# A diffusion step's modulation vectors: from matmuls on TensorE to products on GpSimd and row sums on ScalarE

## The chip, the core and the metric

The kernel runs on one core of a Trainium2 chip. The metric is the device time of one execution in microseconds; a kernel's time is the median of its runs. The trace of the kernel before is one profiled execution on the same kind of core.

## What is computed

One step of a two-layer network over 640 tokens (512 latent, 128 context) of width 1024, all in float32. Each layer begins with six modulation vectors of 1024 numbers, once for the latent tokens (cond = c) and once for the context tokens (cond = c_ctx):

```
m = silu(cond) @ w_ada + b_ada                    # (1024) @ (1024 x 6144)
sh1, sc1, g1, sh2, sc2, g2 = split(m, 6)
h = rms_norm(x) * (1 + sc1) + sh1
x = x + g1 * mixing(h)                            # projection, three branches, W_o
h = rms_norm(x) * (1 + sc2) + sh2
x = x + g2 * swiglu(h)
```

The mixing is one projection of h (6688 columns), gated linear attention, a short convolution, a Fourier mixing, and three gated output projections that are added. The outputs are the normed x of all tokens and the final attention states of the context.

## The kernel before, in words

Activations lie with the channels on the 128 partitions, in tiles of 128 x 640, which come from one pool of 47 "units" (`N_UNITS`). Weights come from HBM in blocks of up to 128 x 1024 into six buffers (`raw`). Float32 products are made as three passes of a rounded type: ScalarE casts a block to its high part (`whi`, line 146), VectorE subtracts for the low part (`wlo`, line 147), and TensorE runs high by high, high by low and low by high. There are three buffers each of `whi` and `wlo`, and `prefetch` prepares two blocks ahead of the one that TensorE works on.

A layer runs through these stages. In the mixing stage 24 `pair`s of projection blocks follow one another; each makes seven products of a Strassen-like scheme out of sums of the weight blocks (VectorE, lines 168 to 174) and adds the results out of PSUM (VectorE, lines 282 to 295). Between the products, generators put in the attention heads. Then come 24 products of the three branches (`gated`, tiles `wb`), the products with W_o (`wo`), and the feed-forward part (`wu`, `wup`, `wd`), ordered by `ffn_order`.

The modulation vectors are made in pieces of 512 columns by `ada`: four loads of 512 KB, each with 8 matmuls in 32-column groups in the code (64 recorded matmuls for a piece), whose stationary operand is `cond` (128 x 32, two columns of it in use). ScalarE copies the result out of PSUM (`adas`, line 368), one transpose on TensorE (line 374) turns it, and VectorE adds the bias (`mod`, line 380). Four pieces, the first two vectors of layer 0, are made in `start`. Of the other 20, each layer's mixing stage makes eight (`ada_after`, at every third pair) and the feed-forward part of layer 0 makes four for layer 1. `ada_flush`, called in `tick_bg` and before the next piece, does the transpose and the bias.

The order on each engine is set by the scheduler of the tile framework from the order of the code, with data dependences, and each engine then runs its instructions in that order: an instruction that waits holds up all that stand behind it on its engine. Loads of weights are issued on SyncE's queue in the order of `make_plan`, at most six ahead.

## Time and profile before

| | us |
|---|---|
| median of three runs | 2059.89 |
| lowest and highest | 2054.49 and 2063.86 |
| profiled execution, device time | 2057.21 |
| span of its trace | 2055.4 |
| TensorE busy in the span | 1996.5 |
| VectorE busy | 1563.0 |
| ScalarE busy | 905.3 |
| GpSimd busy | 18.2 |

[...] "Busy" is the time in which at least one instruction of the engine was on record. On TensorE a record of one matmul is longer than the distance to the next, so the distance between starts says what a matmul costs in a full stream.

### The profile page before, as it was taken

How to read it: one execution, taken by the hardware profiler on the slowest of the kernel's cores; microseconds unless marked ns; L12 is line 12 of the kernel's file. 1: busy time of each engine (PE TensorE's matmuls, PEld its weight loads, DVE VectorE, ACT ScalarE, POOL GpSimd, SP SyncE). 2: the span in 40 equal slices, each digit the busy share in tenths (PEclk: the TensorE clock that was granted, in tenths of full speed). 3: DMA queues.
4: the chain of work that ended last, by engine and by line, in shares of the span. 5: the costliest groups of instructions: out<-in, count | busy, mean ns of one | idle time of the engine just before them, and what ended most of it. 6: DMA issues, size and time to landing. Idle time of an engine off the chain costs nothing.

```text
span 2055.4 us, 36451 instructions
## 1 busy us (share of the span) xinstructions
PE 1996.5 (97%) x14796; PEld 1950.0 (95%) x14796; DVE 1563.0 (76%) x2428; ACT 905.3 (44%) x1419; POOL 18.2 (1%) x52
## 2 busy tenths in 40 slices
PE   5899999999999999999999999999999999999997
PEld 4899999999999999999979999989999999999997
DVE  4778798877667777767677878898675787877876
ACT  3554435445455333333365454444543643333333
POOL 2000000000000000000000000000000000000000
PEclk9999999999999999999999999999999999999999
DMA  8243543554612343332333444335545122222221
GB/s 311 71 167 133 183 139 106 187 186 146 203 56 77 98 126 102 98 124 86 92 122 103 157 163 136 125 125 172 202 162 167 53 69 84 74 89 79 85 71 68
DMA packets 107143, 256.80 MB, mean 125 GB/s; under 512 B 13344, under 2 KB 46304, under 8 KB 106976
## 3 DMA queue, kind: packets, MB, share of 16 engines
q1 hardware_dynamic: 102528, 250.91, 37.3%
q8 instruction: 116, 1.90, 0.4%
q10 hardware_dynamic: 3728, 2.49, 0.4%
q0 software_dynamic: 720, 1.07, 0.1%
q14 instruction: 51, 0.42, 0.1%
HBM read 227.69 MB, written 26.74 MB: 124 GB/s over the span
## 4 chain that ended last, share of the span: by engine, by line
PE 83%; DVE 9%; DMA 4%; ACT 2%; issue 2%; SPq 0%; DVEq 0%; ACTq 0%
PE wd L253 14%; PE wb L253 8%; PE wo L253 3%; DMA raw<-in_w 2%; PE wu L253 2%; DVE wlo L147 2%; PE ada L362 2%; DVE S L737 1%; PE w L253 1%; ACT whi L146 1%; PE o L760 1%; PE w L235 1%; PE w L236 1%; DVE z L295 1%; PE wu L236 1%
## 5 line engine op out<-in xcount | busy, mean ns | idle before, releaser
L146 ACT CAST whi<-raw 128x1024 fp32r<-128x1024 f32 (+2 forms) x368 | 270.0, 734 | 508.2 <-PE wo L253 37.5
L147 DVE TENSOR_TENSOR wlo<-raw,whi 128x1024 fp32r<-128x1024 f32 (+2 forms) x368 | 303.9, 827 | 118.1 <-ACT whi L146 116.5
L146 ACT CAST whi<-sb 128x1024 fp32r<-128x1024 f32 x86 | 90.4, 1051 | 175.6 <-DVE sb L169 55.3
L253 PE MATMUL wd<-ffhi,whi 128*128 128x320 f32 x656 | 149.9, 310 | 0.0
L253 PE MATMUL wd<-ffhi,wlo 128*128 128x320 f32 x656 | 149.4, 309 | 0.0
L253 PE MATMUL wd<-fflo,whi 128*128 128x320 f32 x656 | 149.4, 309 | 0.0
L146 ACT CAST whi<-sc 128x1024 fp32r<-128x1024 f32 x86 | 90.4, 1051 | 96.7 <-PE wd L253 47.7
L497 DVE SCALAR_TENSOR_TENSOR x<-wd,mod,x 128x512 f32<-128x512 f32 x212 | 106.6, 544 | 18.8 <-PE wd L253 18.8
L147 DVE TENSOR_TENSOR wlo<-sc,whi 128x1024 fp32r<-128x1024 f32 x86 | 104.8, 1219 | 18.0 <-ACT whi L146 17.4
L147 DVE TENSOR_TENSOR wlo<-sb,whi 128x1024 fp32r<-128x1024 f32 x86 | 104.8, 1218 | 9.9 <-ACT whi L146 8.3
L253 PEld LDWEIGHTS wd<-ffhi,whi 128*128 128x128 f32 x656 | 109.5, 188 | 0.8 <-ACT ff L405 0.6
L253 PEld LDWEIGHTS wd<-fflo,whi 128*128 128x128 f32 x656 | 109.7, 188 | 0.0
L253 PEld LDWEIGHTS wd<-ffhi,wlo 128*128 128x128 f32 x656 | 109.6, 188 | 0.0
L168 DVE TENSOR_TENSOR sc<-raw 128x512 f32<-128x512 f32 x86 | 59.2, 688 | 41.1 <-DMA raw<-in_w 37.0
L174 DVE TENSOR_TENSOR sc<-raw,sb 128x512 f32<-128x512 f32 x86 | 59.0, 685 | 0.6
L253 PE MATMUL wb<-bhi,whi 128*128 128x320 f32 x256 | 59.3, 312 | 0.0
L169 DVE TENSOR_TENSOR sb<-sc,raw 128x512 f32<-128x512 f32 x86 | 58.9, 684 | 0.5
L170 DVE TENSOR_TENSOR sb<-raw,raw 128x512 f32<-128x512 f32 x86 | 58.8, 684 | 0.0
L253 PE MATMUL wb<-bhi,wlo 128*128 128x320 f32 x256 | 58.6, 309 | 0.0
L253 PE MATMUL wb<-blo,whi 128*128 128x320 f32 x256 | 58.3, 309 | 0.0
L362 PE MATMUL ada<-raw,cond 128*32 128x128 f32 x1536 | 49.6, 280 | 3.6 <-DMA raw<-in_w_ada 2.8
L362 PEld LDWEIGHTS ada<-raw,cond 128*32 128x32 f32 x1536 | 42.0, 112 | 10.2 <-issue 3.6
(2254 smaller groups left out, 6371.8 us busy)
## 6 DMA issues: line engine op xcount, KB each, us to landing
raw<-in_w SPq DMA_DIRECT2D x104, 512.0 KB, 4.2
raw<-in_w_ada SPq DMA_DIRECT2D x96, 512.0 KB, 4.2
raw<-in_wu SPq DMA_DIRECT2D x88, 512.0 KB, 3.6
raw<-in_wd SPq DMA_DIRECT2D x96, 192.0 KB, 2.3
sgd<-z SPq DMA_DIRECT2D x48, 320.0 KB, 2.9
sgl<-sgd SPq DMA_DIRECT2D x48, 320.0 KB, 3.6
raw<-in_wb SPq DMA_DIRECT2D x48, 256.0 KB, 2.8
raw<-in_wo SPq DMA_DIRECT2D x16, 512.0 KB, 3.6
```

The source lines that it names most:

```text
L146: self.nc.scalar.copy(hi[:, 0:n], src)
L147: self.nc.vector.tensor_sub(lo[:, 0:n], src, hi[:, 0:n].bitcast(F32))
L168: nc.vector.tensor_add(sc[:, 0:512], a21, a22)
L169: nc.vector.tensor_sub(sb[:, 0:512], sc[:, 0:512], a11)
L170: nc.vector.tensor_sub(sb[:, 512:1024], a11, a21)
L174: nc.vector.tensor_sub(sc[:, 512:1024], a12, sb[:, 0:512])
L235: nc.tensor.matmul(o, lh, rh, start=start, stop=False)
L236: nc.tensor.matmul(o, lh, rl, start=False, stop=False)
L253: nc.tensor.matmul(o[h], w[:, sl], rhs[kb][h][part], start=(kb == 0 and first), stop=(kb == nk - 1 and last))
L295: nc.vector.tensor_add(zv[:, 3:1:-1], pv(pd), zv[:, 3:1:-1])
L362: self.nc.tensor.matmul(o[32 * j:32 * j + 32], self.cond[:, kb, :], r[:, k, j], start=(kb == 0), stop=(kb == KB - 1))
L497: self.nc.vector.scalar_tensor_tensor(seg(xv), seg(v), g[:, j, i:i + 1], seg(xv), ALU.mult, ALU.add)
```

## The change

The two vectors that `start` makes stay as they were. All others are made anew. A piece is now 128 columns (one load of 512 KB) and lies differently: the 128 partitions are four quarters of the 1024 input rows times 32 output columns, and along a partition lie four column groups of 256 input rows each. For each piece, in two halves of 512 numbers, GpSimd multiplies the weights with silu(cond), once for latent into a new unit (`adp`) and once for context in place, and ScalarE runs a copy over each 256 numbers of a row with a running sum (`accum_out`). When the eight pieces of a vector are done, four small matmuls with a 0/1 matrix (`quarters`, 128 x 32, 16 columns of data) add the four quarters, and VectorE adds the bias for all eight blocks at once. There are 24 pieces in each mixing stage, one at every pair; eight in each branch stage, one at every third product; and 16 in the feed-forward part of layer 0. A piece thus has 4 GpSimd products and 8 ScalarE sums, and 80 pieces have 320 and 640; there are 10 vectors with 4 matmuls each. The flush of a finished vector stands at the next step, no longer in `tick_bg`. The pool has 46 units, and two constants are loaded at the start (`condr`, 256 KB, on ScalarE's queue with one more Silu; `quarters`, 16 KB, on GpSimd's).

```diff
@@ -43,7 +43,7 @@
 BRANCHES = [1, 0, 2]
-N_UNITS = 47
+N_UNITS = 46
 Z_BUFS = 2
@@ -61,10 +61,10 @@
     if phase == "mix":
-        seq = [(l, v, m) for v in (G1, SH2, SC2, G2) for m in range(2)]
-        return seq[i // 3:][:1] if i % 3 == 1 else []
-    seq = [(1, v, m) for v in (SC1, SH1) for m in range(2)]
-    return seq[i // 4 - 1:][:1] if l == 0 and i % 4 == 0 and 4 <= i < 20 else []
+        return [(l, (G1, SH2, SC2)[i // KB], i % KB)]
+    if phase == "branch":
+        return [(l, G2, i // 3)] if i % 3 == 0 else []
+    return [(1, (SC1, SH1)[(i - 2) // KB], (i - 2) % KB)] if l == 0 and 2 <= i < 2 + 2 * KB else []
 
@@ -219,7 +219,6 @@
             f()
-        self.ada_flush()
         self.step(self.gens)
@@ -338,6 +337,11 @@
         self.act(self.cond, self.cond, AF.Silu)
+        self.condr = cp.tile([P, 2, 256], F32, name="condr")
+        nc.scalar.dma_start(self.condr, a["condr"])
+        self.act(self.condr, self.condr, AF.Silu)
+        self.quarters = cp.tile([P, 32], F32, name="quarters")
+        nc.gpsimd.dma_start(self.quarters, a["quarters"])
         self.par = []
@@ -382,18 +386,42 @@
 
-    def ada(self, pieces):
-
-        for piece in pieces:
-            ps = self.psum("ada")
-            u = self.ada_make(ps, [piece])
-            self.ada_flush()
-            self.ada_last = ps, [piece], u
+    def ada_step(self, l, phase, i):
+
+
+        nc = self.nc
+        self.ada_flush()
+        for piece in ada_after(l, phase, i):
+            k = piece[2]
+            raw = self.take(("adb", *piece))
+            if k == 0:
+                self.part = self.cp.tile([P, 4, KB, 2], F32, tag="part", name=self.name("part"), bufs=2)
+            for h in range(2):
+                w = raw[:, h * 512:h * 512 + 512].rearrange("p (g k) -> p g k", g=2)
+                u = self.unit(cols=512, s="adp").rearrange("p (g k) -> p g k", g=2)
+                for i, o in enumerate((u, w)):
+                    nc.gpsimd.tensor_mul(o, w, self.condr[:, i:i + 1].to_broadcast([P, 2, 256]))
+                    for g in range(2):
+                        nc.scalar.activation(o[:, g], o[:, g], AF.Copy, accum_out=self.part[:, 2 * h + g, k, i:i + 1])
+            if k == KB - 1:
+                self.ada_last = piece[0], piece[1], self.part
 
     def ada_flush(self):
-        if self.ada_last:
-            self.ada_end(*self.ada_last)
+        if self.ada_last is None:
+            return
+        nc = self.nc
+        l, v, part = self.ada_last
         self.ada_last = None
+        ps = self.psum("adf")
+        for g in range(4):
+            nc.tensor.matmul(ps[32 * g:32 * g + 32, 0:2 * KB], self.quarters, part[:, g].rearrange("p k i -> p (k i)"), start=True, stop=True)
+        p = self.par[l]
+        mv = p["mod"][:, v]
+        with self.soon():
+            nc.vector.tensor_add(mv, ps[:, 0:2 * KB].rearrange("p (k i) -> p k i", i=2), p["b_ada"][:, v])
+        for w, A, norm in ((SC1, "A1", "norm1"), (SC2, "A2", "norm2")):
+            if v == w:
+                nc.vector.scalar_tensor_tensor(p[A], mv, 1.0, p[norm], ALU.add, ALU.mult)
 
@@ -904,7 +932,11 @@
                 for q in range(4):
-                    plan.append((("ada", l, v, n, q), "raw", [a["w_ada"][l, v * 2 + n, q]]))
+                    plan.append((("ada", l, v, n, q), "raw", [a["w_ada"][v * 2 + n, q]]))
+
+        def adb(*step):
+            for l, v, k in ada_after(*step):
+                plan.append((("adb", l, v, k), "raw", [a["w_adb"][l, v, k]]))
 
@@ -917,10 +949,11 @@
                 w1p(l, n, m)
-                ada(ada_after(l, "mix", i))
-            for b in BRANCHES:
+                adb(l, "mix", i)
+            for n, b in enumerate(BRANCHES):
                 for j in range(KB):
                     full(("wb", l, b, j), a["wb"][l, b, j])
+                    adb(l, "branch", n * KB + j)
             for j in range(KB):
@@ -950,6 +983,7 @@
         self.act(s, s, AF.Sigmoid)
+        self.ada_step(l, "branch", BRANCHES.index(b) * KB + j)
         if b == BRANCHES[0]:
@@ -1053,7 +1087,7 @@
                 self.gens.append(heads())
-            self.ada(ada_after(l, "mix", i))
+            self.ada_step(l, "mix", i)
         self.drain()
@@ -1075,6 +1109,7 @@
             self.gated(l, 2, j, fr, y, yhl)
+        self.ada_flush()
         return [yhl[j] for j in range(KB)]
@@ -1132,7 +1167,7 @@
                 fs.setdefault(ci, []).append(both(*u))
-                self.ada(ada_after(l, "ffn", i))
+                self.ada_step(l, "ffn", i)
                 del t, u
@@ -1209,7 +1244,11 @@
     out["wo"], out["wu"], out["wd"] = _blocks(g["w_o"]), _blocks(g["w_up"]), _blocks(g["w_down"])
-    out["w_ada"] = c(g["w_ada"].reshape(NL, 4, 2, P, 12, 512).transpose(0, 4, 1, 3, 2, 5).reshape(NL, 12, 4, P, 1024))
+    wa = g["w_ada"]
+    out["w_ada"] = c(wa[0, :, 0:2048].reshape(4, 2, P, 4, 512).transpose(3, 0, 2, 1, 4).reshape(4, 4, P, 1024))
+    out["w_adb"] = c(wa.reshape(NL, 4, 256, 6, KB, 4, 32).transpose(0, 3, 4, 1, 6, 5, 2).reshape(NL, 6, KB, P, 1024))
+    out["condr"] = c(np.stack([np.repeat(z.reshape(4, 256), 32, 0) for z in (g["c"][0].reshape(D), g["c_ctx"].reshape(D))], 1))
+    out["quarters"] = c(np.tile(np.eye(32, dtype=np.float32), (4, 1)))
     return out
```

## Rows read from the trace of the kernel before

**Rows 1.** The page: busy time, and busy tenths in 40 slices of the span.
```profile
PE 1996.5 (97%) x14796; PEld 1950.0 (95%) x14796; DVE 1563.0 (76%) x2428; ACT 905.3 (44%) x1419; POOL 18.2 (1%) x52
...
PE   5899999999999999999999999999999999999997
...
PEclk9999999999999999999999999999999999999999
```

**Rows 2.** Windows by stage: mixing, branches, feed-forward of layer 0; mixing of layer 1.
```profile
core 0: us, PE busy (x) PEld busy (x) DVE busy (x) ACT busy (x) POOL busy (x), PEclk, DMA share, GB/s
...
77.00:446.00 369.00, 359.55 (x2888) 347.83 (x2887) 306.00 (x450) 174.35 (x266) 3.66 (x13) 1.00 0.43 146
446.00:545.00 99.00, 99.00 (x699) 98.94 (x698) 72.16 (x115) 53.63 (x101) 0.00 (x0) 1.00 0.51 170
...
625.00:1011.00 386.00, 385.60 (x2830) 383.83 (x2829) 291.75 (x439) 139.98 (x199) 0.00 (x0) 1.00 0.33 99
...
1086.00:1454.00 368.00, 358.95 (x2893) 347.16 (x2892) 305.25 (x448) 173.89 (x266) 3.66 (x13) 1.00 0.44 147
```

**Rows 3.** Timeline of TensorE around one piece: start us, us, engine, line.
```profile
392.14 0.31 PE L236 MATMUL w1p_24d<-tlo,whi 128*128 128x320 f32 x1
392.29 0.31 PE L237 MATMUL w1p_24d<-thi,wlo 128*128 128x320 f32 x1
392.53 1.95 PE L362 MATMUL ada<-raw,cond 128*32 128x128 f32 x64
394.41 0.41 PE L235 MATMUL w1p_26a<-hhl,whi 128*128 128x320 f32 x1
394.66 0.31 PE L236 MATMUL w1p_26a<-hhl,whi 128*128 128x320 f32 x1
```

**Rows 4.** The same around one transpose of a piece.
```profile
156.58 0.27 PE L374 MATMUL ada<-ident,adas 128*128 128x128 f32 x1
156.78 0.48 PE L720 MATMUL u<-v,koT 64*128 64x128 f32 x2
```

**Rows 5.** GpSimd's groups: line, op, shapes, count | busy us, mean ns.
```profile
L663 POOL MEMSET scanm<- 128x640 f32 x2 | 1.3, 636 | 805.1 <-DVE tlo L318 805.1
...
masks.py:199 POOL TENSOR_SCALAR_AFFINE_SELECT ident<-ident 128x128 f32<-128x128 f32 x1 | 0.3, 309 | 0.1
...
L665 POOL MEMSET scanm<- 64x10 f32 x2 | 0.2, 110 | 0.1
```

**Rows 6.** Windows of the mixing stage for VectorE's lines 282, 285, 290, 295 alone.
```profile
77.00:446.00 369.00, 19.61 (x24) 1.00 0.43 146
77.00:446.00 369.00, 11.66 (x24) 1.00 0.43 146
77.00:446.00 369.00, 19.64 (x24) 1.00 0.43 146
77.00:446.00 369.00, 18.82 (x23) 1.00 0.43 146
```

**Rows 7.** VectorE's groups: one input against two inputs in SBUF, 320 columns each.
```profile
L482 DVE TENSOR_TENSOR hhl<-hx,hhl 128x320 fp32r<-128x320 f32 x64 | 30.3, 487 | 6.1 <-ACT hhl L481 5.6
...
L479 DVE CAST hhl<-hx 128x320 fp32r<-128x320 f32 x32 | 10.0, 320 | 1.3 <-ACT hx L602 1.3
```

**Rows 8.** What VectorE waited for in the mixing stage: us in total, times, longest.
```profile
DVE wlo L147 <- ACT whi L146: 21.6, 21, 2.7
DVE sc L168 <- DMA raw<-in_w: 17.5, 8, 3.6
```

**Rows 9.** ScalarE's groups: nearest rows to a sum over 256 columns.
```profile
L877 ACT COPY fb<-pa 128x256 f32<-128x256 f32 x8 | 2.9, 369 | 2.1 <-PE pa L237 2.1
...
L879 ACT COPY fr<-pa 128x1 f32<-128x1 f32 x8 | 1.4, 177 | 0.0
```

**Rows 10.** Groups of the whole span: casts and subtractions of full weight blocks.
```profile
L146 ACT CAST whi<-sb 128x1024 fp32r<-128x1024 f32 x86 | 90.4, 1051 | 175.6 <-DVE sb L169 55.3 <-DVE sb L170 35.6 <-PE wd L253 29.3
...
L147 DVE TENSOR_TENSOR wlo<-sb,whi 128x1024 fp32r<-128x1024 f32 x86 | 104.8, 1218 | 9.9 <-ACT whi L146 8.3 <-PE wu L253 1.4
```

More of the change, by code (lines that the diff above doesn't have):

```diff
@@ L936, in make_plan @@
                     plan.append((("wup", l, i), "pair", [g, u]))
-                ada(ada_after(l, "ffn", i))
+                adb(l, "ffn", i)
             ci = len(FF_CHUNKS) - 1
```

## Prediction

> **What bounds the kernel now.** I read the page first: TensorE is busy in 97% of the span, at 9 tenths or more in all but the first two and the last of 40 slices, and its granted clock is at 9 tenths or more throughout [rows 1], 1.00 or the upper level of 2.4 GHz in the stages that the change touches [rows 2], so the clock has no time to give. Then the windows by stage: in the mixing stage of layer 0 TensorE has work in 359.6 of 369.0 us, in the branch stage in all 99.0, in the feed-forward part in 385.6 of 386.0 [rows 2]. Matmul records overlap, so I looked in the timeline whether the stream is really full: starts of full matmuls lie 0.15 us apart and records last 0.31 [rows 3]. TensorE is the bound, and what leaves its queue is saved one for one as long as nothing else becomes later. The next engine is VectorE: 306.0 us of the 369.0 in the mixing stage, 83%, against 73% among the branches and 76% in the feed-forward part [rows 2]. ScalarE has room everywhere (174.4 of 369.0), GpSimd is empty.
>
> **What is removed.** One piece on TensorE: the last matmul ahead of it starts at 392.29, the second one behind it at 394.66. Between them lie 2.37 us, of which two ordinary steps of 0.15 would be there anyway, so 2.07 us go [rows 3]. A transpose takes 0.20 from its start to the next [rows 4]. 20 pieces by 2.27 us are 45.4 us: 18.2 in each mixing stage and 9.1 in the feed-forward part of layer 0. VectorE and ScalarE lose a small addition and a small copy for each piece; I leave them out, as they would only shorten queues that are long for other reasons. PSUM buffers that a piece held until its flush come free sooner, and the four loads in a row are spread out; VectorE's 17.5 us of waiting for weights in the mixing stage [rows 8] shrink, but TensorE stood idle there for only 9.4 us in all [rows 2], which bounds that gain.
>
> **What is added to TensorE.** Ten flushes, each of four matmuls in the code, which the trace would record as eight, since the old ones are recorded twice as well. 64 such matmuls have 1.95 us from first start to last end [rows 3], so one more costs 0.03, and a flush costs the latency of 0.27 [rows 4] plus 8 by 0.03, 0.5 us. All ten: 5 us, two of them in each mixing stage. The sums that a flush reads are one step old in the mixing stage, some 15 us, so I take no wait there.
>
> **What is added to GpSimd, and what it does to VectorE.** 4 products of 128x512 for a piece: 96 in a mixing stage, 32 among a layer's branches, 64 in the feed-forward part of layer 0. No row shows a product on GpSimd. A memset takes 0.636 us for 640 columns and 0.110 for 10 [rows 5], that is 0.11 and 0.00083 a column: a product at that pace, one result a step, takes 0.54 us, and if its two inputs are read one after the other 0.97. Four times the row of 128x128 that reads and writes is 1.24 [rows 5]. I take 1.1 us, halfway between the last two, since a product reads two inputs; 0.54 and 1.24 stay as the ends. (The Trainium skill, GPSIMD Engine Reference, section Elementwise — side-by-side cycle accounting, gives 4497 ns for an addition of 2048 columns; a quarter is an estimate of 1.12 us, and by it the sum below would be 3 us higher.)
>
> GpSimd itself has time for this: 96 by 1.1 are 105.6 us in 369. The question is whether VectorE goes on beside it. The lowest cost is zero. The highest is that VectorE stands for each whole product. The nearest rows: with one input in SBUF VectorE does 320 columns in 0.320 us, with two inputs it takes 0.487 [rows 7]. The one-input form is a third faster column for column, which I read as two ways into SBUF, both used for the one input in the first case and one for each input in the second; a third reader has to find a way beside these two, or take one. I take it that a product stops VectorE when VectorE's operation has two inputs in SBUF, and not when one input is in PSUM. (The Trainium skill, SBUF — State Buffer, section Who interferes with whom, speaks against this change: a VectorE instruction with two SBUF inputs contends with a GpSimd instruction that reads SBUF, for the whole instruction. No run so far shows it; by that rule the sum is the one that follows, without it it is the first rival's.)
>
> In the mixing stage the additions out of PSUM (lines 282 to 295) make 69.7 us [rows 6], which leaves 236 of VectorE's 306 us, 64% of the stage, in operations that mostly have two inputs in SBUF: `wlo`, the sums of weight blocks, the scans and state updates. So of 105.6 us of products 64%, 67.6 us, stop VectorE. Its work becomes 306.0 + 67.6 = 373.6 us, more than TensorE's 369.0 - 18.2 + 1.0 = 351.8. VectorE is then what ends last, and of its idle time I keep the part that is its own loop with ScalarE, 21.6 us of waiting for `whi` [rows 8]; the rest (weights, TensorE) I let go. The stage takes 395.2 us, 26.2 more than before. The mixing stage of layer 1 is the same but for 1 us (305.3 + 67.6 + 21.6 against 368.0 [rows 2]): 26.5 more.
>
> Among the branches: 35.2 us of products, at 64% 22.5, and VectorE comes to 94.7 of 99.0 us, still under TensorE. I cost it at zero, with 8.4 us a layer as the end if every product stopped VectorE (72.2 + 35.2 = 107.4), plus 1 us a layer for two flushes. In the feed-forward part even with a full stop VectorE has 291.8 + 70.4 = 362 us, under TensorE's 377; there the gain of 9.1 stays, less 1.0 for two flushes.
>
> **ScalarE.** 8 sums of 128x256 for a piece, at 0.369, the row of a copy of that shape [rows 9], 2.95 us; if reading out the sum is an instruction of its own, 0.177 more each, 4.4. In the mixing stage that is 71 to 105 us on top of 174, 279 of 395 at most: hidden by amount. By order it need not be: a sum that waits for its product holds up the casts behind it (second rival). At the start, the load of `condr` and its Silu lie ahead of the first weight block, for which ScalarE waits longer anyway; zero. SyncE issues as many loads as before, 16 + 80 in place of 96; a buffer of `raw` is held until the sums of its piece are done, and one of six held for some 10 us of a 15 us pair is no more than four in a row before. GpSimd's memsets for the heads queue behind at most four products, 4.4 us or twice that with stops; I take that as hidden.
>
> **Sum.** 2055.4 + 26.2 + 26.5 - 8.1 + 2.0 = 2102.0 us of span; with the 1.8 us around it 2104 us. The profiled execution (2057.2) lies 2.7 below the median of the runs, so against the median the change is 44 us slower within about 3. A measurement of this kernel can tell some 0.5%, 10 us, from no change.
>
> **Rivals.** *VectorE goes on undisturbed.* Then TensorE stays the bound everywhere: 2055.4 - 45.4 + 5.0 + 1.8 = 2017 us, 2% faster. For it speaks that no row shows a stop, and that GpSimd's place in the shares is empty. The deciding point between this and the forecast is how long a product stops VectorE on average: the mixing stage stays at its 369.0 us when VectorE's work with its 21.6 us of waiting leaves 41.4 us for 96 products, 0.43 each; I reckon with 0.70.
>
> *GpSimd gets its turn mostly in VectorE's gaps and beside its additions from PSUM.* At half my price, 33.8 us a stage, the mixing stages take some 361 us, 7.6 less each, and the kernel is at 2055.4 - 15.2 - 8.1 + 2.0 + 1.8 = 2036; between that and the forecast lies no change.
>
> *ScalarE's order.* If the sums of a piece stand together in ScalarE's queue, they hold it for four products with a VectorE operation of about 0.7 ahead of each, 7.2 us. TensorE can spare that for a while: two blocks of 24 matmuls ahead, 7.0 us, less a cast of 1.05 and a subtraction of 1.22 [rows 10], 4.7 us. The other 2.5 us, 48 times in the mixing stages, are 120 us: with TensorE's saving, 2017 + 120 = 2137. Without stops the products take 4.4 us and this costs nothing, so it only decides where the forecast's mechanism holds. Against it: sums need not stand together, and the two delays partly cover each other.
>
> **How the numbers follow.** Forecast, VectorE as the bound of the mixing stages: 0.50, from 2067 (0.52 us a product, 8 more a stage than before) to 2130 (0.84 us a product, 39 more). ScalarE's order on top: 0.10, 2130 to 2160. Undisturbed: 0.22, 2014 to 2025. Gaps: 0.18, 2025 to 2067, half of it under 2049. Slower by over 0.5%: 0.50 + 0.10 less 0.02 for the edge: 0.58. Faster: 0.22 + 0.09 = 0.31. The rest, 0.11, is within 0.5%. As cases of both signs hold most of the chance, the range takes in both: 2015 to 2138, which leaves out the upper part of ScalarE's case and the edges, under 2 in 10. The forecast's own range is 2067 to 2130.
>
> **What the profile after would show.** Right: VectorE's two-input rows beside GpSimd's products longer than their 0.68 and 1.22 us, or gaps ahead of them; VectorE over 95% busy or stopped in the mixing stages and TensorE with idle time that ends at `wlo` or `z`; mixing stages near 395 us, the feed-forward part of layer 0 near 378. Products of 1.0 to 1.2 us. Wrong: unchanged durations on VectorE and mixing stages near 352 (first rival), or TensorE's waits ending at `whi` while ScalarE waits for products (third). A product much under 1 us, or an order in which products meet VectorE's idle time, would make the prediction wrong.

## The result and the profile after

The change makes the kernel slower: 2203.67 us (median of four runs, 2203.32 to 2205.48) against 2059.61 before, a ratio of 1.0708 (95% interval 1.069 to 1.0725). The forecast was 2104, with 2138 as the upper end: the sign was right, the size was not. The profiled execution has a span, from its first to its last instruction, of 2201.1 us.

The page of after, the line of busy times, answers to [rows 1]:

```profile
PE 2025.9 (92%) x13576; PEld 1964.9 (89%) x13576; DVE 1757.2 (80%) x2415; ACT 1147.6 (52%) x2680; POOL 562.6 (26%) x373
```

TensorE has 1220 records fewer than before and yet is busy for 29 us longer. The place is seen in the windows by stage (mixing and branches of layer 0, feed-forward part of layer 0, mixing of layer 1; the columns of [rows 2]):

```profile
77.34:480.69 403.35, 362.70 (x2387) 348.70 (x2385) 372.82 (x442) 243.89 (x628) 168.71 (x107) 0.94 0.35 116
480.69:601.68 120.99, 106.79 (x708) 103.95 (x709) 93.04 (x123) 79.65 (x242) 53.32 (x34) 0.94 0.59 197
...
703.34:1132.45 429.11, 403.97 (x2672) 397.34 (x2671) 317.59 (x452) 196.38 (x463) 104.92 (x64) 0.98 0.31 100
...
1172.47:1577.45 404.98, 361.98 (x2386) 348.29 (x2385) 372.41 (x437) 243.36 (x628) 165.70 (x108) 0.94 0.35 116
```

The same stages of the kernel before, cut in the same way, from the first matmul of a stage to the first of the next (the feed-forward window of [rows 2] begins 21 us before that part and ends 35 us before its end):

```profile
76.75:446.10 369.35, 359.90 (x2890) 348.18 (x2889) 306.25 (x451) 174.70 (x267) 3.66 (x13) 1.00 0.43 146
446.10:544.31 98.21, 98.21 (x694) 98.15 (x693) 71.47 (x115) 52.84 (x101) 0.00 (x0) 1.00 0.52 171
646.22:1046.16 399.94, 398.47 (x2916) 396.45 (x2915) 297.54 (x455) 147.36 (x212) 0.00 (x0) 1.00 0.35 107
1086.19:1453.81 367.62, 358.57 (x2890) 346.78 (x2889) 305.06 (x448) 173.51 (x265) 3.66 (x13) 1.00 0.44 148
```

Against these the mixing stages take 34.0 and 37.4 us more, the branch stages 22.8 and 21.8, the feed-forward part of layer 0 29.2; the other stages are within 1 us of before. VectorE's busy time grew by 66.5 us in the mixing stage of layer 0, and the granted clock, 1.00 in these stages before, is 0.94 and 0.98, so TensorE now runs for part of them at its lower level of 1.2 GHz.

The groups of after (count | busy us, mean ns | idle before, and what ended it) show which operations became longer:

```profile
L403 POOL TENSOR_TENSOR raw<-raw,condr 128x512 f32<-128x512 f32 x160 | 277.6, 1754 | 1.9
L403 POOL TENSOR_TENSOR adp<-raw,condr 128x512 f32<-128x512 f32 x160 | 270.1, 1703 | 1021.9 <-PE wd L252 178.5 <-PE w L252 131.1 <-DVE tlo L317 128.4
...
L147 DVE TENSOR_TENSOR wlo<-raw,whi 128x512 fp32r<-128x512 f32 x150 | 133.0, 887 | 15.2 <-ACT whi L146 13.5 <-DMA sgl<-sgd 1.6
...
L405 ACT ACTIVATE adp<-adp 128x256 f32<-128x256 f32 x320 | 129.4, 406 | 23.0 <-POOL adp L403 23.0
...
L405 ACT ACTIVATION_READ_ACCUMULATOR adp<-adp 128x1 f32 x320 | 60.2, 188 | 0.0
...
L992 DVE TENSOR_TENSOR y<-y,sgl 128x640 f32<-128x640 f32 x32 | 35.6, 1112 | 0.3
...
L991 DVE TENSOR_TENSOR sgl<-wb,sgl 128x640 f32<-128x640 f32 x32 | 26.0, 814 | 2.7 <-issue 1.9 <-PE wb L252 0.8
```

The first `wlo` row in the kernel before:

```profile
L147 DVE TENSOR_TENSOR wlo<-raw,whi 128x512 fp32r<-128x512 f32 x150 | 102.5, 683 | 15.5 <-ACT whi L146 14.7 <-DMA dft<-in_dft 0.7
```

`wlo` of 512 columns, two inputs in SBUF, went from 0.68 to 0.89 us; `y`, both inputs in SBUF, takes 1.11, while `sgl` of the same size, with one input in PSUM, takes 0.81 in the last line (0.82 for both before); `x<-wd` (one input in PSUM) is 0.75 before and after. A product takes 1.70 to 1.75 us on average. A sum is two instructions, 0.406 and 0.188 us.

One stretch of the feed-forward part shows all of it at once. The timelines of GpSimd, VectorE and ScalarE around 762 us (start, us, engine, line; in brackets the idle time before):

```profile
760.71 1.72 POOL L403 TENSOR_TENSOR adp<-raw,condr 128x512 f32<-128x512 f32 x1 [33.40 <-PE wd L252]
762.50 2.16 POOL L403 TENSOR_TENSOR raw<-raw,condr 128x512 f32<-128x512 f32 x1
764.62 1.30 POOL L403 TENSOR_TENSOR adp<-raw,condr 128x512 f32<-128x512 f32 x1
766.00 1.31 POOL L403 TENSOR_TENSOR raw<-raw,condr 128x512 f32<-128x512 f32 x1
767.26 2.55 POOL L403 TENSOR_TENSOR adp<-raw,condr 128x512 f32<-128x512 f32 x2
769.74 4.12 POOL L403 TENSOR_TENSOR raw<-raw,condr 128x512 f32<-128x512 f32 x2
```

```profile
760.45 0.81 DVE L317 TENSOR_TENSOR fflo<-ff,ffhi 128x640 fp32r<-128x640 f32 x1
...
761.45 2.06 DVE L147 TENSOR_TENSOR wlo<-sb,whi 128x1024 fp32r<-128x1024 f32 x1
...
769.24 1.24 DVE L1166 TENSOR_TENSOR ff<-z,ff 128x640 f32<-128x640 f32 x1 [4.81 <-ACT ff L433]
770.41 2.30 DVE L147 TENSOR_TENSOR wlo<-sc,whi 128x1024 fp32r<-128x1024 f32 x1
```

```profile
762.46 0.42 ACT L405 ACTIVATE adp<-adp 128x256 f32<-128x256 f32 x1 [1.92 <-POOL adp L403]
...
764.70 0.42 ACT L405 ACTIVATE raw<-raw 128x256 f32<-128x256 f32 x1 [1.33 <-POOL raw L403]
...
768.16 0.40 ACT L276 COPY s<-wup_6a 128x320 f32<-128x320 f32 x1
768.47 0.74 ACT L433 ACTIVATE ff<-z 128x640 f32<-128x640 f32 x1
```

While VectorE stands (4.81 us, up to 769.24) a product takes 1.30 us, its length alone. Otherwise they take turns. The first product starts 0.55 us before `fflo` ends and takes 1.72, 0.42 longer; `wlo`, 1.22 without products [rows 10], starts 0.98 before that product ends and takes 2.06, 0.84 longer; the second product starts 1.01 before `wlo` ends and takes 2.16, 0.86 longer. So the one that comes second stands until the other is done, but for some 0.14 us, and a record of 1.72 or 2.06 us holds that wait. The whole trace shows the same. Of 77 `wlo` that began with more than 0.15 us of a product still to run, 74 were longer by the rest of that product less 0.11 to 0.16 us; of 87 products that began with as much of a `wlo` to run, 86 were longer in the same way; the 24 `wlo` that began ahead of a product were not longer.

The first product had waited 33.40 us for its output, a unit of the pool that the last down product gave back; then eight products run back to back. ScalarE's sums wait for them, and `s` and the Silu of `ff` stand behind the sums.

TensorE's timeline 20 us later shows what a wait leaves behind:

```profile
788.04 0.41 PE L236 MATMUL wup_7a<-hhl,wlo 128*128 128x320 f32 x1 [1.81 <-DVE wlo L147]
...
788.58 0.36 PE L236 MATMUL wup_7a<-hhl,wlo 128*128 128x320 f32 x1
788.75 0.47 PE L234 MATMUL wup_7a<-hhl,whi 128*128 128x320 f32 x1
789.01 0.47 PE L235 MATMUL wup_7a<-hhl,whi 128*128 128x320 f32 x1
```

After 1.81 us without work the starts lie 0.25 us apart once, then 0.14 to 0.17, and 0.27 from 788.75 on: the lower level (the granted clock is 0.50 between 789 and 792).

### The profile page after: what moved, and what is told of

Same layout as the page of the kernel before. It is cut to its first block, busy times and chain, and to the rows that moved or that the text cites. A ratio compares the mean times of both kernels' runs of the same rounds, so it can differ in the third digit from the quotient of the medians.

```text
span 2201.1 us, 35855 instructions
## 1 busy us (share of the span) xinstructions
PE 2025.9 (92%) x13576; PEld 1964.9 (89%) x13576; DVE 1757.2 (80%) x2415; ACT 1147.6 (52%) x2680; POOL 562.6 (26%) x373
## 3 DMA queue, kind: packets, MB, share of 16 engines
q8 instruction: 107, 1.75, 0.3%
## 5 line engine op out<-in xcount | busy, mean ns | idle before, releaser
L403 POOL TENSOR_TENSOR adp<-raw,condr 128x512 f32<-128x512 f32 x160 | 270.1, 1703 | 1021.9 <-PE wd L252 178.5
L147 DVE TENSOR_TENSOR wlo<-raw,whi 128x1024 fp32r<-128x1024 f32 (+2 forms) x368 | 343.4, 934 | 87.3 <-ACT whi L146 85.3
L403 POOL TENSOR_TENSOR raw<-raw,condr 128x512 f32<-128x512 f32 x160 | 277.6, 1754 | 1.9
L405 ACT ACTIVATE raw<-raw 128x256 f32<-128x256 f32 x320 | 129.1, 405 | 24.9 <-POOL raw L403 24.5
L405 ACT ACTIVATE adp<-adp 128x256 f32<-128x256 f32 x320 | 129.4, 406 | 23.0 <-POOL adp L403 23.0
L147 DVE TENSOR_TENSOR wlo<-sb,whi 128x1024 fp32r<-128x1024 f32 x86 | 115.7, 1345 | 18.2 <-ACT whi L146 18.1
L147 DVE TENSOR_TENSOR wlo<-sc,whi 128x1024 fp32r<-128x1024 f32 x86 | 114.7, 1334 | 11.9 <-ACT whi L146 11.9
L170 DVE TENSOR_TENSOR sb<-raw,raw 128x512 f32<-128x512 f32 x86 | 73.9, 859 | 0.0
L174 DVE TENSOR_TENSOR sc<-raw,sb 128x512 f32<-128x512 f32 x86 | 72.8, 846 | 0.2
L169 DVE TENSOR_TENSOR sb<-sc,raw 128x512 f32<-128x512 f32 x86 | 70.9, 824 | 0.5
```

What stands on the lines that cost most here:

```text
L147: self.nc.vector.tensor_sub(lo[:, 0:n], src, hi[:, 0:n].bitcast(F32))
L169: nc.vector.tensor_sub(sb[:, 0:512], sc[:, 0:512], a11)
L170: nc.vector.tensor_sub(sb[:, 512:1024], a11, a21)
L174: nc.vector.tensor_sub(sc[:, 512:1024], a12, sb[:, 0:512])
L403: nc.gpsimd.tensor_mul(o, w, self.condr[:, i:i + 1].to_broadcast([P, 2, 256]))
L405: nc.scalar.activation(o[:, g], o[:, g], AF.Copy, accum_out=self.part[:, 2 * h + g, k, i:i + 1])
```

## Experiments: what the parts cost

Theory A: a product on GpSimd lengthens VectorE's operations with two inputs in SBUF, and that sets the time. Theory B: sums that wait for products hold ScalarE's queue, with casts and copies behind them. Theory C: ScalarE's amount. Later Theory D: it is the bursts of products.

**Neither products nor sums.** This is called the floor: what is left is the saving on TensorE, with the loads and flushes of the changed kernel.

```diff
+                nc.gpsimd.memset(self.part, 0.0)
...
-                u = self.unit(cols=512, s="adp")...
-                for i, o in enumerate((u, w)):
-                    nc.gpsimd.tensor_mul(o, w, ...)
-                    for g in range(2):
-                        nc.scalar.activation(...)
+                pass
```

> Left out: all products on GpSimd and all sums on ScalarE, so the ten moved modulation vectors are the bias alone; loads, flushes and everything else as in the changed kernel. This is the floor, the saving on TensorE alone. All theories: 2017 us (the prediction's first rival, 45 us saved less 5 for flushes), flush waits of nearly zero, granted clock 0.99. If it lies above 2035, the price is in the loads, the buffers or the flushes, and no theory on products and sums is needed for that part.

2024.88 us (2023.97 to 2025.04; ratio 0.984, 0.9818 to 0.9861). So TensorE's saving is there, 8 us less than forecast. Windows of the floor, same stages (layer 1's mixing stage left out):

```profile
75.86:432.87 357.01, 346.71 (x2386) 338.02 (x2385) 306.29 (x444) 173.44 (x259) 3.96 (x15) 0.98 0.42 139
432.87:532.15 99.28, 99.18 (x710) 98.43 (x709) 71.86 (x117) 52.52 (x100) 0.31 (x2) 1.00 0.60 196
...
634.51:1026.44 391.93, 390.46 (x2673) 389.59 (x2671) 299.00 (x452) 146.71 (x208) 0.30 (x2) 1.00 0.34 106
```

**Sums alone, and products alone.**

```diff
-                    nc.gpsimd.tensor_mul(o, w, ...)
-                        nc.scalar.activation(o[:, g], o[:, g], AF.Copy, accum_out=...)
+                        nc.scalar.activation(o[:, g], w[:, g], AF.Copy, accum_out=...)
```

> Left out: the products; ScalarE's 640 sums stay and run over the raw weights, so the vectors are sums of weights. Theory A (a product on GpSimd stops VectorE): 2017 to 2035, since no product is there. Theory B (ScalarE's queue is held while a sum waits for its product): also near the floor, 2020 to 2045, since no sum waits. Theory C (the amount on ScalarE, 0.59 us a sum with its read-out, 4.75 us a piece, delays casts and copies by itself): 2100 to 2150, half or more of the 185 us between floor and changed kernel.

> Left out: the 640 sums (the parts are zero); the 320 products stay in place. Theory A (products stop VectorE): stays high, 2120 to 2200, VectorE's two-input rows 10 to 30% longer as in the changed kernel, granted clock in the mixing stage below 0.97. Theory B (order of ScalarE): falls to the floor plus 0 to 30 us, 2017 to 2050, even if VectorE's rows stay long. Theory C: the same as B.

Sums alone: 2042.19 us (0.992, 0.9897 to 0.9943), 17 over the floor. Products alone, without the two lines of the sum and with the parts set to zero: 2173.28 (1.0561, 1.0541 to 1.0582), 148 over the floor. Both are 179; some 13 belong to neither alone. C falls; the products are the cost. Mixing of layer 0 and feed-forward part with products alone:

```profile
76.75:487.06 410.31, 366.10 (x2386) 353.51 (x2385) 374.01 (x443) 171.29 (x257) 165.16 (x109) 0.93 0.35 118
...
696.13:1112.89 416.76, 401.11 (x2672) 396.26 (x2671) 333.18 (x452) 144.56 (x207) 106.26 (x66) 0.98 0.32 102
```

**What about a product costs: writing, reading one input, or reading two.** First a write-only stand-in of about the same length (three memsets, 1.24 us in all), then a multiplication by a constant.

```diff
-                    nc.gpsimd.tensor_mul(o, w, ...)
+                    nc.gpsimd.memset(o, 2e-4)
+                    nc.gpsimd.memset(o, 1e-4)
+                    nc.gpsimd.memset(o[:, 0, 0:128], 1e-4)
```

> Changed: each product is replaced by three memsets on GpSimd of 512, 512 and 128 columns, about the same 1.3 us of GpSimd, but nothing is read there; the sums wait for them as for the products and run over constants. Theory A (GpSimd's reading stops VectorE): 2030 to 2080, VectorE's rows back to 0.68 and 1.22 us. Theory B (sums wait for GpSimd in ScalarE's queue, whatever GpSimd does): 2130 to 2200, VectorE's rows short but ScalarE still waiting for GpSimd some 40 us and TensorE for `s` and `wlo`. If writing takes VectorE's place as reading does, the rows stay long and nothing is told apart.

```diff
-                    nc.gpsimd.tensor_mul(o, w, ...)
+                    nc.gpsimd.tensor_scalar(o, w, 0.01, None, op0=ALU.mult)
```

> Changed: each product becomes a multiplication by a constant on GpSimd, 512 columns with one input instead of two; it reads the weights and writes where the product did, and the sums follow as before, so the vectors are scaled sums of weights. If any GpSimd instruction that reads SBUF stops VectorE: VectorE's rows stay long (subtractions of 512 columns at 0.80 us or more, 0.68 alone) and the time 2140 to 2200, in proportion to the instruction's length. If only one with two inputs does: rows back to 0.68 and 1.22 us and 2045 to 2060, as with the write-only memsets (2051).

Write-only: 2050.57 us (0.996, 0.9946 to 0.9974), `wlo` of 512 columns back at 0.684 us:

```profile
L407 ACT ACTIVATE raw<-raw 128x256 f32<-128x256 f32 x320 | 130.8, 410 | 94.8 <-POOL raw L404 86.5 <-DVE S L767 2.7 <-POOL raw L405 1.8
...
L147 DVE TENSOR_TENSOR wlo<-raw,whi 128x512 fp32r<-128x512 f32 x150 | 102.6, 684 | 15.2 <-ACT whi L146 14.7
```

And yet ScalarE's sums waited longer for GpSimd here than in the changed kernel (86.5 us in the first row alone, 48 there in all). That speaks for A and against B. The whole is 26 us over the floor, 8 over the sums alone. One input: 2094.25 us (1.0182, 1.016 to 1.0203), between the two expectations. Its rows, and its mixing and feed-forward windows:

```profile
L147 DVE TENSOR_TENSOR wlo<-raw,whi 128x512 fp32r<-128x512 f32 x150 | 109.4, 730 | 16.8 <-ACT whi L146 16.4 <-DMA sgl<-sgd 0.4
```

```profile
77.24:447.15 369.91, 349.76 (x2387) 338.75 (x2385) 323.10 (x444) 244.37 (x631) 158.84 (x108) 0.98 0.39 131
...
656.92:1077.04 420.12, 399.24 (x2672) 392.58 (x2671) 300.83 (x452) 196.79 (x463) 106.92 (x64) 0.99 0.32 102
```

GpSimd is nearly as busy as in the changed kernel (159 us of the stage against 169), and VectorE is longer by 17 us than in the floor in place of 67: 0.18 us an instruction against 0.71 (95 and 94 of them lie in the stage). So it is the reading, and two inputs far more than one: 48 of 97 `wlo` that began with more than 0.15 us of a one-input instruction to run were longer, and the 97 by 0.16 us on average, against 74 of 77 and 0.77 us beside the products. But the feed-forward part is 420 us with VectorE hardly longer (300.8): there A is not the whole story.

**Half of the products.**

```diff
-                    nc.gpsimd.tensor_mul(o, w, ...)
+                    if i == 0:
+                        nc.gpsimd.tensor_mul(o, w, ...)
```

> Changed: only the latent products are made (160 of 320); the context sums run over the raw weights. All 640 sums stay. The prediction's picture (VectorE has some 41 us to spare in a mixing stage, and products cost nothing until that is used up; half of them stop VectorE for about 33 us a stage): 2042 to 2070, near the sums alone (2042). If a product costs wherever it falls, because what counts is the few us around it and not the stage's sum: halfway, 2123, 2100 to 2140.

2101.12 us (1.0212, 1.0188 to 1.0236): 59 over the sums alone, where all products cost 162. More than the threshold picture of the prediction and less than half; the time lies at the lower end of the second expectation. In the mixing stage of layer 0 VectorE is longer by 31 us in place of 67, and the stage takes 15 us more than with the sums alone (359.9):

```profile
76.78:451.64 374.86, 353.64 (x2386) 343.28 (x2385) 336.88 (x442) 244.38 (x630) 91.28 (x62) 0.97 0.37 125
```

VectorE stands for 38 us here, for 31 with all products: its waiting for others shrinks slowly as its work grows. So the first 31 us on VectorE are not free, though the prediction reckoned with 41 to spare; whether a smaller share would be, no run shows.

## Experiments: why the stages with room lost most

**Sums one step later.** The sums of a piece are issued at the next step, a vector is flushed one step later.

```diff
-                    for g in range(2):
-                        nc.scalar.activation(o[:, g], ...)
+                    self.ada_sums.append((o, self.part, h, k, i))
```

> Complete computation. The eight sums of a piece are issued one step later than its products, and a vector is flushed one step later still, so that ScalarE finds its products done. The products alone gave 2173, the sums alone 17 us over the floor of 2025, both 2204. Theory B (a sum that waits for its product holds ScalarE's queue): the waiting goes, 2170 to 2190, ScalarE's wait for GpSimd under 10 us in place of 48, the branch stage back from 121 to some 110 us. Theory A (VectorE is stopped by products, ScalarE's order costs nothing of its own): 2195 to 2210, ScalarE's wait for GpSimd gone all the same.

2191.37 us (1.0653, 1.0632 to 1.0674). A miss for both: ScalarE still waited 46 us for products, so the edit didn't do what it was for. Products that start late would be late at the next step, too. The feed-forward part fell to 408 us, the mixing stages rose to 408 and 412:

```profile
703.32:1111.32 408.00, 395.47 (x2673) 389.62 (x2671) 318.91 (x452) 195.44 (x463) 111.01 (x64) 1.00 0.33 105
```

**Buffers of their own for the products**, without and with the sums one step later:

```diff
-N_UNITS = 46
+N_UNITS = 44
-                u = self.unit(cols=512, s="adp")...
+                u = self.wp.tile([P, 512], F32, tag="adp", ..., bufs=2)...
```

> Complete computation. The products that go into a new buffer get two buffers of their own (128x512) in place of units of the pool, which shrinks from 46 to 44. In the feed-forward part of the changed kernel a product into a unit waits up to 37 us for the end of a down product, and then two pieces run their eight products in one burst of 13 us. Theory D (it is the bursts that cost where no engine is full): pieces run one by one as their weights land, the feed-forward part of layer 0 falls from 429 to 400 to 412 us, the mixing stages stay within 8 us, in all 2165 to 2190. Theory A in its plain form (only the amount on VectorE counts): no change, 2195 to 2210, and slower than that if 44 units are too few.

> Complete computation: two buffers of their own for the products and a pool of 44 (which gave 2242, with ScalarE waiting 293 us for products and VectorE 14 us less busy in a mixing stage), and now also the sums of a piece one step later. Theory B (what lengthened that kernel is ScalarE held by sums whose products wait for their weights): ScalarE's wait for GpSimd under 60 us, the feed-forward part of layer 0 at 395 to 408 us, the mixing stages at 395 to 408, in all 2150 to 2190, less than the changed kernel's 2204. If 44 units are what lengthened it: 2220 or more with the waits gone.

2241.72 (1.0896, 1.088 to 1.0913) and 2243.49 us (1.0891, 1.087 to 1.0913), both missed. The feed-forward part did fall to 414 and 416 us, but the mixing stages rose to 424 to 426. There VectorE has less to do than in the changed kernel (358.6 us in the mixing stage of layer 0), and the products' wait went from units to weights:

```profile
L403 POOL TENSOR_TENSOR adp<-raw,condr 128x512 f32<-128x512 f32 x160 | 256.7, 1625 | 1136.4 <-DMA raw<-in_w_adb 995.4 <-ACT sqh L455 82.0 <-ACT whi L146 29.9
```

ScalarE waited 293 and 284 us for products in the two kernels, and several of TensorE's longest waits are for `s`, up to 5.0 us each. Two things changed at once (44 units, and another order of the sums among ScalarE's other work), so these two kernels settle nothing on the bursts. That waits of this size in ScalarE's queue cost is likely from TensorE's waits for `s`, but not shown apart.

**Products and sums that don't depend on each other.** Both remain, no sum waits for a product.

```diff
-                    nc.gpsimd.tensor_mul(o, w, ...)
-                        nc.scalar.activation(o[:, g], o[:, g], AF.Copy, ...)
+                    nc.gpsimd.tensor_mul(u, w, ...)
+                        nc.scalar.activation(self.junk, w[:, g], AF.Copy, ...)
```

> Changed: products and sums no longer depend on each other. Each product goes into the new unit, each sum runs over the raw weights into a scratch tile, so all 320 products and 640 sums are there at their full cost, but no sum waits for a product; the vectors are sums of weights. Products alone gave 2173 (branches 106, feed-forward part of layer 0 417, mixing 410 and 406), products and dependent sums 2204 (121, 429, 403 and 405). If the rest of 14 us over products alone and sums alone, and the branches' and the feed-forward part's above all, is ScalarE waiting for products: branches 105 to 110, feed-forward 410 to 419, in all 2170 to 2190. If the lengthened VectorE and ScalarE's amount do it without any waiting: branches 117 to 123, feed-forward 424 to 432, 2195 to 2210.

2213.17 us (1.0746, 1.0722 to 1.077), no faster than the changed kernel; the feed-forward part keeps 426 us. But ScalarE's queue was not freed. Its sums now wait for weights, 121 us in the whole kernel and 65 in this part, where the sums of the changed kernel wait for products for 32 (us in total, times, longest):

```profile
ACT junk L406 <- DMA raw<-in_w_adb: 65.0, 12, 10.1
```

So this kernel doesn't settle Theory B in this part. The products alone do: with no sum at all the part takes 417 us, 25 of the 37 over the floor, so B is not the main cause there. In the branches the stage goes from 121 and 120 to 113 and 114, between the two expectations, so of the 21 us over the floor about 7 are sums that wait; W_o behind them takes 60.6 and 59.0 in place of 57.1, so some 4 us a layer are left as the gain. The mixing stages take 416 us each, 12 more than in the changed kernel, with the same 373 and 372 us on VectorE.

**The same, with a product tile of their own.** Nothing reads it, so no product waits for a unit.

```diff
-N_UNITS = 46
+N_UNITS = 45
-                u = self.unit(cols=512, s="adp")...
+                u = self.prods...
```

> Changed: as with independent products and sums (2213), but the products go into one tile of their own that nobody reads, so they wait for no unit of the pool and start when their weights have landed; the pool has 45 units. All 320 products and 640 sums stay, and the vectors are sums of weights. Theory D (bursts of eight or more products behind a wait of 30 us for a unit are what makes the feed-forward part lose 37 us where VectorE has 25% to spare): that part falls from 426 to 395 to 408, the mixing stages, where units come free all the time, stay at 400 to 416; in all 2160 to 2195. Theory A (any product beside VectorE's chain costs, in a burst or alone): feed-forward 418 to 430, 2200 to 2220.

2178.78 us (1.0586, 1.0569 to 1.0604). The feed-forward part, without and with the edit (one fence for each kernel):

```profile
709.25:1135.59 426.34, 401.43 (x2673) 393.77 (x2671) 330.80 (x452) 193.17 (x431) 109.21 (x64) 0.99 0.31 100
```

```profile
715.72:1109.11 393.39, 390.73 (x2672) 389.59 (x2671) 342.43 (x457) 194.51 (x420) 88.58 (x53) 1.00 0.34 106
```

Now 393.4, 1.5 over the floor, with VectorE longer by 43 us than there. VectorE's lengthening costs next to nothing in this stage when pieces come one by one as their weights land; the stage is 34 over the floor when two or three pieces come at once, after a wait for a unit. Theory D holds here as far as this: the wait for a unit and what follows from it is what costs. What follows are the bursts and, with them, weights that land late (the sums' wait for weights fell from 65 to 14.5 us); how much is due to each isn't shown. Not all of the 33 us is a gain: some pieces moved into the stages next to it, which are 7 and 5 us longer than in the floor, so from the first `wu` to the next mixing stage it is 491 us against 510, and 477 in the floor. That is 19 us of 33. The mixing stages stay at 414 and 408, as expected where VectorE itself is short.

**The work on VectorE itself**: product and row sum in one instruction.

```diff
-                    nc.gpsimd.tensor_mul(o, w, ...)
                     for g in range(2):
-                        nc.scalar.activation(o[:, g], ...)
+                        nc.vector.tensor_tensor_reduce(out=o[:, g], in0=w[:, g], in1=self.condr[:, i], ..., accum_out=...)
```

> Complete computation, on another engine: VectorE makes product and row sum in one instruction (128x256, eight a piece); GpSimd and ScalarE do nothing for the vectors. By VectorE's rows of two inputs (0.68 us for 512 columns, 1.22 for 1024) one of 256 should take 0.42, 3.3 us a piece, 80 us more in a mixing stage, against 67 us by which the products on GpSimd lengthen VectorE's busy time there. If a stop on VectorE is all that GpSimd's help brings (theory A): about as long as the changed kernel, mixing stages 395 to 420, but the feed-forward part of layer 0 near its floor of 392 to 400, as no queue of ScalarE waits, branches 105 to 115; in all 2130 to 2180. If GpSimd's work is cheaper for VectorE than doing it: over 2204.

2130.36 us (1.0346, 1.0327 to 1.0365), 73 less than the changed kernel, with GpSimd and ScalarE relieved of all of it. The total is at the lower end of the first expectation; its stages were missed (mixing 387 and 382, branches 118 and 117, feed-forward part 403):

```profile
L404 DVE CUSTOM_DVE_ANT_0 adp<-raw,condr 128x256 f32<-128x256 f32 x320 | 122.8, 418 | 0.1
...
L404 DVE DVE_READ_ACCUMULATOR2_ANT part<- 128x1 f32 x640 | 51.7, 81 | 0.0
```

```profile
76.81:463.96 387.15, 357.86 (x2355) 341.68 (x2354) 360.92 (x790) 170.50 (x255) 3.66 (x13) 0.96 0.37 124
...
76.81:463.96 387.15, 64.31 (x352) 0.96 0.37 124
```

The second of the two windows holds VectorE's line 404 alone. In the mixing stage of layer 0 these instructions occupy VectorE for 64.3 us, 22 pieces, 2.9 us each; the products on GpSimd lengthened it by 66.5 us for 94 products, 2.8 us a piece. GpSimd's help saves VectorE next to nothing, and ScalarE's sums and GpSimd's late products come on top.

**Only where VectorE has room.** The kernel before, with two and then four of layer 1's vectors on VectorE in the feed-forward part of layer 0, into a scratch tile.

```diff
-                self.ada(ada_after(l, "ffn", i))
+                self.row_step(l, i)
```

> Complete computation. The kernel before, except that the two vectors made in the feed-forward part of layer 0 (SC1 and SH1 of layer 1) are made there by VectorE, product and row sum in one instruction into a scratch tile, 16 pieces of about 3.3 us. VectorE has 298 of 392 us in that part and comes to some 351. If only amounts count, the whole saving of the part stays: 8 us, 2049 to 2053 against the kernel before at 2057 to 2060. If a burst of 3.3 us on VectorE already makes TensorE wait, as products do: 2055 to 2070.

> Complete computation. As with two vectors on VectorE in the feed-forward part of layer 0 (2051), but four: SC1, SH1, G1 and SH2 of layer 1, 32 pieces over 20 steps, some steps with two. VectorE gained 2.3 us of busy time a piece there, so it comes to about 298 + 74 = 372 of 392 us. The mixing stage of layer 1 loses four of its eight pieces on TensorE, 2.27 us each. If room in the stage is what counts: the part stays at 392 to 396, the mixing stage falls by 6 to 9, in all 2042 to 2048. If two pieces in one step, 4.6 us of VectorE, are more than the weights' lead hides: the part grows by 10 or more and the kernel is no faster than with two vectors, 2050 to 2065.

2051.43 us (0.9966, 0.9954 to 0.9978) and 2045.93 us (0.9933, 0.9916 to 0.995): a little faster than the kernel before, by 0.3 and 0.7%, and so faster than either kernel. The feed-forward part with two vectors, and with four:

```profile
648.55:1040.68 392.13, 390.65 (x2673) 389.58 (x2671) 335.51 (x670) 146.75 (x209) 0.00 (x0) 1.00 0.35 106
```

```profile
650.16:1046.44 396.28, 393.36 (x2688) 390.29 (x2687) 374.69 (x925) 146.07 (x208) 0.00 (x0) 1.00 0.39 126
```

With four vectors VectorE is busy for 375 of 396 us and the stage is 4 us over the floor; layer 1's mixing stage takes 357.1, 10.5 less than before. With the change VectorE is busy for 318 us of the feed-forward part, and that is 37 over the floor.

## Why the prediction was wrong

By its own steps, with what each was worth (forecast, measured; us more than before):

| step | forecast | measured |
|---|---|---|
| saving on TensorE, feed-forward part (floor) | -8.1 | -8.0 |
| saving on TensorE, mixing stages (floor) | -17.2 each | -12.3 and -14.2 |
| VectorE's busy time, mixing of layer 0 | +67.6 | +66.5 |
| VectorE's own idle time, mixing | 21.6 | 30.5 and 32.6 |
| mixing stages | +26.2 and +26.5 | +34.0 and +37.4 |
| branch stages | +1 each | +22.8 and +21.8 |
| feed-forward part of layer 0 | -8.1 | +29.2 |

**Mixing: mechanism right, one term too small.** VectorE's busy time came out within 1 us of the forecast, 372.8 against 373.6. That the price of a product, 0.70 us forecast and 0.71 measured, came out so close was luck: it was 64% of 1.1 us, and it is 55% of the 1.30 that a product takes by itself. (The 1.73 us on record hold the product's own waiting.) The Trainium skill's page "SBUF — State Buffer", section "Who interferes with whom", names the operations rightly: two-input rows are longer, rows with an input from PSUM and rows beside write-only memsets are not. The page calls the shared ports an exclusive lock, and the prediction took this as a stop for a whole instruction; the trace agrees, as 74 of 77 `wlo` waited out the product beside them.

The term that was mis-sized is the idle time kept: 21.6 us of waiting for `whi` was taken as all that remains, and 30.5 and 32.6 remained. These 9 and 11 us are all of the 8 and 11 by which the two stages were missed. Of the time that remained only 10.0 and 10.6 us are waits for `whi`; the rest are other waits for ScalarE, TensorE and VectorE's own results. Nor is it a fixed loop: with VectorE busy for 372 to 374 us the mixing stage of layer 0 took 403 in the changed kernel, 410 with products alone, and 414 and 416 in the kernels with independent sums. Of TensorE's waits there that the trace names, some 21 us end at VectorE and 15 at ScalarE, so VectorE is the larger part of what ends last but not all of it.

**Branches and feed-forward part: this is the step that failed.** "I cost it at zero" and "there the gain of 9.1 stays" compared shares of a whole stage. VectorE's amount in the branches was even right (94.7 forecast, 93.0 measured), but a stage of 99 us does not hide it: of the 14.2 us in which TensorE stands idle in the branches of layer 0, 8.7 end at VectorE's `y` and 4.2 at the sums of the flush. What counts, it seems, is how long VectorE and ScalarE are late at the moment, against the two blocks ahead of TensorE. These two steps make 43 and 37 of the 100 us by which the forecast was low. Nothing in the text asked when a product would run. In the feed-forward part its output is a unit of the pool, units come back only at the end of the down products, and two or three pieces then run together; with that wait taken away the stage is back within 1.5 us of its floor, and with the stages beside it within 14, where they were 33 over with it. In the branches a part stays open: sums alone cost 3 us, products alone 7, both without dependence 14, with it 21; why 14 and not 10, wasn't measured further.

**"The clock has no time to give"** was true of the kernel before and no argument for the one after. In the feed-forward part the 37 us over the floor are 23.7 us of TensorE's idle time (25.1 against 1.5) and 13.5 us by which it is busy longer with the same matmuls (404.0 against 390.5). In the branches it is 14.1 and 7.6. The lower level is a part of the longer busy time: a granted clock of 0.98 over 429 us makes up at most some 9 of the 13.5, one of 0.94 over 121 us some 7 of the 7.6. The rest isn't clock: with the sums one step later the granted clock of the feed-forward part is 1.00, and TensorE is still busy for 5.0 us longer than in the floor. The floor's mixing stage lost some of its saving in this way: granted clock 0.98, busy time down by 13 us, where by the prediction's count 18.2 left TensorE's queue and 1 us came in.

**The flush, "I take no wait there"**, was wrong: the last sums of a vector are not done where ScalarE is behind. TensorE's waits over the whole of after (us in total, times, longest), 11 us of the first row in the mixing stages and 8 in the branches; the second row is the branches' own:

```profile
PE adf L417 <- ACT raw L405: 19.2, 6, 5.0
...
PE wb L252 <- DVE y L989: 16.9, 6, 5.8
```

**Rivals.** *VectorE undisturbed* fell with the rows of VectorE; its 2017 us as a floor was low by 8. *GpSimd in the gaps* fell too: it had half of 0.70 us a product, and 0.71 was measured. A product does wait until VectorE's operation is done, but the next one then waits for the product. *ScalarE's order* had its mechanism in the trace (sums ahead of `s` and `ff`, 1.92 and 1.33 us of waiting) and its time, 2137, was nearest; but the products keep 148 of the 179 us over the floor with no sum at all, so it isn't the cause of the size. Its price in the branches is some 4 to 7 us a layer. Sums alone, forecast as hidden by amount, cost 17 us in all.

## What to carry to other kernels

Before work goes to GpSimd beside a busy VectorE, price the product by what it adds to VectorE's two-input operations; here that was 2.8 us a piece, about the 2.9 that VectorE needs to do the work itself with a product-and-sum instruction. A stage's share of busy time says nothing on when added work runs: follow what its output buffer and its inputs wait for, and count how many pieces then come at once against the lead of the engine that sets the end. Work done in VectorE's own queue, spread by its inputs' arrival, could fill a stage to 95% at a cost of 4 us.

## What the runs showed of the hardware

- A GpSimd product with two inputs in SBUF and a VectorE operation with two inputs in SBUF run one after the other: whichever comes second waits for the rest of the first, less some 0.13 us (74 of 77 and 86 of 87 cases in after). A long record of either is a wait, not slower work.
- GpSimd's multiplication of 512 columns by a second tensor takes 1.30 us alone; by a constant, with one input, 1.49 us, in this row of the one-input kernel, beside which VectorE stood. The shorter one, with two inputs, costs VectorE four times as much (0.71 against 0.18 us).

```profile
716.94 1.49 POOL L403 TENSOR_SCALAR adp<-raw 128x512 f32<-128x512 f32 x1
```

- A write-only instruction of GpSimd costs VectorE's two-input operations next to nothing (`wlo` 0.684 us beside memsets).
- A running sum on ScalarE has a read-out of its own, 188 ns beside the 406 of the copy; on VectorE it is 81 beside 418.
- TensorE's steps of 0.15 us a matmul came back after a wait of 1.81 us and fell to 0.27 only later, at 788.75, while it was working.
